# Moving VectorE's waits for transfers behind other work, and the scaling of the normed outputs to ScalarE, in a hybrid short-conv and gated DeltaNet layer

## The chip, the core and the metric

The kernel runs on one core of one Trainium2 chip. The metric is the device time of one execution in microseconds (us). A measurement of this kernel can tell differences of about 0.3% from no change.

## What is computed

One layer of a streaming encoder is applied to 4096 frames of a new stream and to 32 frames of a running stream. The reference, cut to what matters:

```python
h    = rmsnorm(x, ln_pre)                       # 4096 x 1024
proj = h @ w_in                                 # columns [B_a | C_a | X_a | Z_a | qkv | Z_g | a_dec | b_beta]
y_a  = b_a * causal_dwconv3(c_a * x_a) * silu(z_a)          # group A, 512 channels
q, k, v = split(silu(causal_dwconv4(qkv)))                  # group B, 4 heads x 128
q, k = l2norm(q), l2norm(k)
g    = -exp(a_log) * softplus(a_dec + dt_bias); beta = sigmoid(b_beta)
S_t  = exp(g_t) (I - beta_t k_t k_t^T) S_{t-1} + beta_t k_t v_t^T;   o_t = q_t^T S_t / sqrt(128)
y_g  = rmsnorm(o, gdn_norm_w) * silu(z_g)
y    = x + rmsnorm(concat(y_a, y_g) @ w_out, ln_post)
```

The outputs are both y, and the last inputs of the convolutions and the last state S of both streams.

## The kernel before, in words

The work has three stages. The first one (up to about 1400 us) goes over the stream in 16 blocks of 256 frames and makes group B. The second makes group A for eight pairs of blocks with a Winograd-like product of 2x2 blocks. The third multiplies by w_out and normalises. All matrix products use weights and activations split in two f16 parts, three products for one.

The first stage is written as a loop over groups, one block each. A group has eight steps (two pairs of k, q, v and z columns each, in the order k, k, q, q, v, v, z, z), and every step two slots, so a group has 16 slots. In a step TensorE makes two products of 24 matmuls (`proj`), ScalarE copies them out of PSUM (L430), ScalarE makes the first tap of the convolution (L434), VectorE the other three (L436, six instructions in a pair), and ScalarE the silu (L437). Other work of the block and of the block before it is put into numbered slots (`at_slot`, L858 on):

- `norm_qk`, `gram` and `subst` of the block at slots 7 to 12: the Gram products, their decayed copies M and at (L490, L491), a trip through DRAM (`lad`, `la`), the reciprocal of the diagonal on VectorE (L539 to L541), and a forward substitution of 31 steps on GpSimd (L546 to L551). Its result goes by 16 transfers (`Tc`, L560) into `merge`, at slots 26 to 31, that is in the next group.
- `gates` of the next block at slots 9, 10 and 13, and `decays` of the next block at the end of the group: a transfer of the cumulated gates to all partitions (`gB`, L397), one subtraction that waits for it (L398), eight instructions that make the exponents (L409), and their exponential on ScalarE (L404, L410).
- `xprep` of the next block at slot 2: norm, split and transposition of x (L271 to L299).
- `rec_a` and `rec_b` of the block before, slots 24 to 44: the recurrence over the state (L654, L674) and the output. `rec_b` adds the two halves of o (L687), squares it with an accumulated sum on ScalarE (L691), makes the norm's factor (L693, L694 on VectorE, a power on GpSimd at L137, called `rsqrt`, and the product with cc on VectorE at L696), scales o on VectorE (L697), transposes it on TensorE (`om`) and multiplies by the gate on VectorE (L703).
- `prep_a` at the fourth step: the weights of group A are made ready, a pair of columns in two halves. The first half (`scaled`) loads two tiles of w_in into `xtw` (L205), multiplies by ln_pre (L206, VectorE, waits for the transfer), takes absolute values on ScalarE (L208), adds them up (L213), sums over partitions on TensorE (`gL`), and scales by a power of two (L223 to L232). The second half (`out`, L749, L750) makes the sums and differences of the quarters on ScalarE and GpSimd.
- `prep_t` at the fourth step of groups 5, 6, 8, 9 and 11 to 14: sums of activations for the second stage, on GpSimd and ScalarE (L769 to L784).

Groups 1 to 13 call `prep_a` once, groups 4, 7 and 10 twice. First halves fall into groups 1, 3, 4, 6, 7, 9, 10 and 12, second halves into 2, 4, 5, 7, 8, 10, 11 and 13.

The order of the instructions on each engine is not the written one: a scheduler sorts them by dependence, by priority (`first` raises it) and by its own estimate of durations. `tc.issue_after(ins)` adds one more rule, that the instructions of the block that run on the engine of `ins` come behind it. Each engine then runs its list in order. All transfers are issued by SyncE. The transfers of `xtw` share five buffers (`xt`) with those of x.

Of the kernel before, what the change touches and what calls it, by code (L numbers as in the profile page):

```python
# [14 lines left out]
ALU = mybir.AluOpType  # L15
# [34 lines left out]
def hybrid_kernel(  # L50
# [139 lines left out]
    def scaled(cts, n=P, urow=None):  # L190


        ws = wa["w"] = []
        first = cts[0] >= 16
        nm = f"{cts[0]}"
        L = bank("r", [P, 2, P], f"L{nm}")[:, :len(cts), :n] if first else None
        sums = []
        e = te([P, 2, P], I32, "we", 1, nm)[:, :len(cts), :n]
        for i, ct in enumerate(cts):
            if 20 <= ct < 24:  # L200
                w = tl([P, D], F32, "v" if ct < 22 else "zg", 2, f"w{ct}")
            else:
                w = te([P, D], F32, "xt", NXT, f"w{ct}")
            w = w.rearrange("p (k c) -> p k c", k=KT)[:, :, :n]
            dma(w, w_in[:, ct * P:ct * P + n].rearrange("(k p) c -> p k c", p=P))  # L205
            (V if ct in VLN or not first else G).tensor_tensor(w, w, bc(lnp, 2, n), ALU.mult)  # L206
            ab = te([P, D], BF16, "jb", 1, f"w{ct}").rearrange("p (k c) -> p k c", k=KT)[:, :, :n]
            A.activation(ab, w, AF.Abs)  # L208
            kn = KT
            if not first:  # L210
                ab2 = e[:, i, 0:P // 2].bitcast(BF16)
                for kn, o in ((4, ab[:, 0:4]), (2, ab[:, 0:2]), (1, ab2.unsqueeze(1))):
                    V.tensor_tensor(o, ab[:, 0:kn], ab[:, kn:2 * kn], ALU.add)  # L213
                sums.append(ab2)
            for k in range(kn if first else 0):
                T.matmul(L[:, i], ones16, ab[:, k, :], start=k == 0, stop=k == kn - 1)
            ws.append(w)
        if not first:
            yield
            L = bank("g", [P, 2, P], f"L{nm}")  # L220
            for i in range(2):
                T.matmul(L[:, i], ones16, sums[i], start=True, stop=True)
        V.tensor_scalar(e.bitcast(F32), L, 2.0 ** -100, None, ALU.max)  # L223
        V.tensor_scalar(e, e, EXP_MASK, None, ALU.bitwise_and)
        if urow is not None:
            V.tensor_scalar(urow.bitcast(I32), e[:, 0], 1, float(-(WS + HS) * BIT), ALU.mult, ALU.add)
        else:
            u = te([1, 2, P], I32, "wu", 1, nm)
            V.tensor_scalar(u, e[0:1], 1, float(-(WS + HS) * BIT), ALU.mult, ALU.add)
        V.tensor_scalar(e, e, -1, float((254 + WS) * BIT), ALU.mult, ALU.add)  # L230
        for i, w in enumerate(ws):
            V.tensor_tensor(w, w, bc(e[:, i].bitcast(F32), 1, KT), ALU.mult)  # L232
        if not first:
            yield
        if urow is None:
            up = bank("o" if first else "g", [P, 2], f"u{nm}")
            for i in range(2):
                T.matmul(up[:, i:i + 1], u[:, i].bitcast(F32), one1, start=True, stop=True)
            V.tensor_copy(usc[:, cts[0]:cts[0] + 2], up)
# [181 lines left out]
    def qkv_pair(b, c0, dst):  # L421

        n = b["n"]
        pt = bank("pj", [P, 2, NB1], f"{b['id']}_c{c0}")
        proj(b, 16 + c0, pt[:, 0])
        yield
        proj(b, 17 + c0, pt[:, 1])
        u = te([P, 2, 3 + NB1], F32, "u", 2, f"{b['id']}_{c0}")
        V.tensor_copy(u[:, :, 0:3], b["hist"][:, c0:c0 + 2, :])
        A.activation(u[:, :, 3:3 + n], pt[:, :, :n], AF.Copy)  # L430
        V.tensor_copy(b["hist_new"][:, c0:c0 + 2, :], u[:, :, n:n + 3])
        for i in range(2):
            d = dst[:, i]
            A.activation(d, u[:, i, 0:n], AF.Copy, scale=cw[:, 0, c0 + i:c0 + i + 1])  # L434
            for j in range(1, 4):
                V.scalar_tensor_tensor(d, u[:, i, j:j + n], cw[:, j, c0 + i:c0 + i + 1], d, ALU.mult, ALU.add)  # L436
        queued("silu", lambda: A.activation(dst, dst, AF.Silu))  # L437

    def z_pair(b, c0):
# [81 lines left out]
    def subst(b):  # L521
# [14 lines left out]
            dma(la[32 * g:32 * g + nl], b["lad"].rearrange("c h q j i -> (c h q) j i"))  # L536

        rl = sc[:, 448:480]
        V.tensor_scalar(rl, la.rearrange("p a b -> p (a b)")[:, ::33], EPS, None, ALU.add)  # L539
        V.reciprocal(rl, rl)  # L540
        V.tensor_tensor(rl, rl, b["bl"], ALU.mult)  # L541
        G.memset(lt, 0.0)
# [135 lines left out]
    def rec_b(b, c):  # L678

        C = b["C"]  # L680
        nm = f"{b['id']}_{c}"
        sl = slice(c * C, (c + 1) * C)
        o, vn = b["rec"].pop(c)
        po = bank("m", [P, NH, P], f"o{nm}")[:C]
        for h in range(NH):
            T.matmul(po[:, h], b["at"][c][:, h, :C], vn[:, h], start=True, stop=True)
        V.tensor_tensor(o, o, po, ALU.add)  # L687
        so = tl([P, 2, NH], F32, "so", 2, nm)[:C]
        jk = b["at"][c]
        for h in range(NH):  # L690
            A.activation(jk[:, h], o[:, h], AF.Square, accum_out=so[:, 0, h:h + 1])  # L691
        f = so[:, 1]
        V.tensor_tensor(so[:, 0], so[:, 0], b["c2"][:, c], ALU.mult)  # L693
        V.tensor_scalar(so[:, 0], so[:, 0], EPS, None, ALU.add)  # L694
        rsqrt(so[:, 0], f)
        V.tensor_tensor(f, f, b["cc"][:, c], ALU.mult)  # L696
        V.tensor_tensor(o, o, bc(f, 2, P), ALU.mult)  # L697
        yield
        pm = bank("o", [P, NH, P], f"m{nm}")[:, :, :C]
        for h in range(NH):  # L700
            T.transpose(pm[:, h], o[:, h], ident[:C, :C])
        mg = b["zg"][:, :, sl]
        V.scalar_tensor_tensor(mg, pm, gwc, mg, ALU.mult, ALU.mult)  # L703
        if b["s"]:
            dma(mxd_s[:, NH:], mg)
        else:
            o0 = b["o"] + c * C
            dma(mxd[o0 // NB2][:, NH:, o0 % NB2:o0 % NB2 + C], mg)
# [157 lines left out]
    def run_slot(i):  # L866
        for fn in slots.pop(i, ()):
            fn()

    def first(fn, *a):  # L870

        with tc.high_priority(1500):
            fn(*a)
# [59 lines left out]
    for gi, grp in enumerate(groups):  # L933
# [5 lines left out]
        else:  # L939
# [19 lines left out]
            for si, (kind, c0) in enumerate(steps):  # L959
                ps = pair(b, kind, c0)  # L960
                next(ps)
                run_slot(s0 + 2 * si)
                ends(ps)
                run_slot(s0 + 2 * si + 1)
                if si == 3:
                    for _ in range((1 <= gi <= 13) + (gi in (4, 7, 10))):

                        p = prevs[-1]
                        with tc.issue_after(p["subst_end"]):
                            pa = prep_a()  # L970
                            if next(pa, 0) is None:
                                at_slot(s0 + 11, next, pa)
                                at_slot(s0 + 13, ends, pa)
                    if gi in (5, 6, 8, 9, 11, 12, 13, 14):
                        with tc.issue_after(prevs[-1]["subst_end"]):
                            prep_t((5, 6, 8, 9, 11, 12, 13, 14).index(gi))
        if gi + 1 < len(groups):
            decays(groups[gi + 1][0])
        for b in grp:
            if b["last"]:  # L980
                out_hist(b)
# [409 lines left out]
```

## Time and profile before

| | |
|---|---|
| median of 3 runs | 2385.7 us (2382.73 to 2390.21) |
| the profiled execution | 2385.77 us, of which the span of the trace is 2384.1 us |
| TensorE busy | 2141.4 us (90% of the span), 18626 matmuls |
| VectorE, ScalarE, GpSimd busy | 1564.8, 980.3 and 1333.7 us (66%, 41%, 56%) |
| mean granted clock of TensorE | 0.956 of full speed |
| chain of work that ended last | TensorE 15%, other engines 0% |

A matmul's end is modelled in this profile and matmuls overlap, so the busy time of TensorE says less than how many matmuls it starts in a microsecond. A wait is the idle time of an engine ahead of an instruction, put down to what came last.

### The profile page before, as it was taken

To read this page: it belongs to the slowest core of one execution; us is meant where nothing else is said; L and a number is where in the kernel's file an instruction comes from. 1 tells how busy PE (TensorE), PEld (TensorE's weight loads), DVE (VectorE), ACT (ScalarE), POOL (GpSimd) and SP (SyncE) were. 2 spreads that over 40 slices of the span, in tenths; PEclk is the share of its full clock that TensorE was granted. 3 is DMA by queue.
4 is the path that set the end of the run, shared out by engine and by line. 5 is a ranking of instruction groups with operands and counts; after the bars stand their busy time and mean duration, and the time that the engine had idled before them with its cause. 6 is when DMAs were issued, how large, how long until landed. Compare 5 with 4: busy or idle time off the path is not lost. (4 is left out here: it accounts for less than half of the span.)

```text
span 2384.1 us, 48173 instructions
## 1 busy us (share of the span) xinstructions
PE 2141.4 (90%) x18626; PEld 1713.9 (72%) x18626; DVE 1564.8 (66%) x3720; ACT 980.3 (41%) x2513; POOL 1333.7 (56%) x1750
## 2 busy tenths in 40 slices
PE   4676989799889988998899999899999999999998
PEld 3465878687778777877778889788888888444443
DVE  4786877677777786767766655656576656455661
ACT  4454655465556555655565411121221121333331
POOL 4435573656675767566776430674467431466763
PEclk9788999899899999999999999999999999999999
DMA  6344341433334243433342425212211122344441
GB/s 125 46 104 92 87 114 48 78 105 97 91 91 111 87 101 87 115 92 95 80 123 72 148 112 182 84 63 71 89 46 54 45 92 88 113 159 145 136 135 72
DMA packets 257198, 230.81 MB, mean 97 GB/s; under 512 B 111576, under 2 KB 196376, under 8 KB 256968
## 3 DMA queue, kind: packets, MB, share of 16 engines
q1 hardware_dynamic: 256968, 227.73, 33.9%
q8 instruction: 146, 2.39, 0.4%
q14 instruction: 84, 0.69, 0.1%
HBM read 133.09 MB, written 76.74 MB: 88 GB/s over the span
## 5 line engine op out<-in xcount | busy, mean ns | idle before, releaser
L74 PEld LDWEIGHTS <-w 128*128 128x128 f16 x6528 | 624.8, 101 | 117.7 <-POOL w L729 16.9
L74 PE MATMUL pj_c<-hhi,w 128*128 128x256 f16 x3072 | 559.6, 282 | 3.0 <-ACT u L430 3.0
L74 PE MATMUL pj_c<-hlo,w 128*128 128x256 f16 x1536 | 433.4, 282 | 0.0
L74 PEld LDWEIGHTS <-w_a 128*128 128x128 f16 x2880 | 269.5, 98 | 48.0 <-issue 16.0
L74 PEld LDWEIGHTS <-opm 128*128 128x128 f16 x1536 | 149.3, 98 | 176.2 <-issue 0.7
L551 POOL TENSOR_TENSOR lt<-lt 128x112 f32<-128x112 f32 (+29 forms) x496 | 235.4, 475 | 37.0
L436 DVE SCALAR_TENSOR_TENSOR qk<-u,cw,qk 128x256 f32<-128x256 f32 x384 | 238.5, 667 | 9.5 <-ACT qk L434 9.1
L550 POOL TENSOR_TENSOR lt<-la,lt 128x112 f32<-128x112 f32 (+29 forms) x496 | 211.6, 427 | 36.2
L74 PE MATMUL pja<-op,w_a 128*128 128x256 f16 x1536 | 190.0, 273 | 3.1 <-DVE w L1034 1.9
L74 PE MATMUL pj_z<-hhi,w 128*128 128x256 f16 x1024 | 187.9, 281 | 0.0
L74 PE MATMUL ga<-op,w_a 128*128 128x256 f16 x1152 | 147.7, 274 | 10.5 <-DVE w L1034 6.7
L74 PE MATMUL pj_z<-hlo,w 128*128 128x256 f16 x512 | 144.0, 281 | 0.0
L74 PE MATMUL pjo<-w_o,opm 128*128 128x512 f16 x528 | 118.5, 379 | 0.0
L137 POOL TENSOR_TENSOR oss<-oss,mhalf 128x2 f32<-128x2 f32 (+1 forms) x17 | 50.0, 2940 | 114.6 <-DVE oss L1280 114.6
L74 PE MATMUL ro<-w_o,opm 128*128 128x512 f16 x504 | 113.4, 379 | 0.0
L74 PE MATMUL go<-w_o,opm 128*128 128x512 f16 x504 | 113.1, 379 | 0.0
L546 POOL TENSOR_TENSOR la<-la,lt 128x1024 f32<-128x1024 f32 x16 | 38.0, 2374 | 126.9 <-DVE lt L541 103.6
L1034 DVE TENSOR_TENSOR w<-pja,w 128x256 f32<-128x256 f32 x152 | 61.7, 420 | 63.6 <-PE pja L74 61.5
L769 ACT ACTIVATE op<-tsc 128x512 f16<-128x512 f32 x48 | 30.2, 630 | 173.0 <-POOL tsc L775 100.0
L750 POOL TENSOR_TENSOR hl<-xtw,hl 128x512 f16<-128x512 f32 x56 | 66.7, 1208 | 61.9 <-ACT hl L749 61.9
L436 DVE SCALAR_TENSOR_TENSOR v<-u,cw,v 128x256 f32<-128x256 f32 x192 | 98.6, 549 | 3.0 <-ACT v L434 2.8
L437 ACT ACTIVATE qk<-qk 128x512 f32<-128x512 f32 x64 | 40.2, 633 | 142.8 <-DVE qk L436 142.8
(650 smaller groups left out, 4791.4 us busy)
## 6 DMA issues: line engine op xcount, KB each, us to landing
xt<-in_x_prompt_dram SPq DMA_DIRECT2D x32, 512.0 KB
mx<-mxd SPq DMA_DIRECT2D x16, 1024.0 KB
op<-hTd SPq DMA_DIRECT2D x30, 512.0 KB
xtw<-in_w_in_dram SPq DMA_DIRECT2D x28, 512.0 KB
wad<-hl SPq DMA_DIRECT2D x56, 256.0 KB
gB<-gd SPq DMA_DIRECT2D x16, 516.0 KB
hTd<-hhi SPq DMA_DIRECT2D x16, 512.0 KB
hTd<-hlo SPq DMA_DIRECT2D x16, 512.0 KB
```

The source lines that it names most:

```text
L74: return self.queue(nc.tensor.matmul(*a, **k))
L137: G.tensor_tensor(y, x, mhalf[:x.shape[0], :x.shape[-1]], ALU.pow)
L436: V.scalar_tensor_tensor(d, u[:, i, j:j + n], cw[:, j, c0 + i:c0 + i + 1], d, ALU.mult, ALU.add)
L437: queued("silu", lambda: A.activation(dst, dst, AF.Silu))
L546: E.tensor_tensor(la, la, bc(rl, 1, 32), ALU.mult)
L550: E.tensor_tensor(tm, bc(la[:, j, j + 1:32], 2, w), bc(lt[:, j, 0:w], 1, r), ALU.mult)
L551: last = E.tensor_tensor(lt[:, j + 1:32, 0:w], lt[:, j + 1:32, 0:w], tm, ALU.subtract)
L750: G.tensor_tensor(hl[:, 1], src, hl[:, 0], ALU.subtract)
L769: A.activation(d[i][0], t, AF.Copy)
L1034: V.tensor_tensor(dst, p, src, ALU.add)
```

## The change

Four things are changed. In `scaled`, both transfers are issued first, and for the weights of group A the generator then yields, so that the multiplication by ln_pre and the sums come in a later slot: 13 instead of the place in step four, behind the block's last Gram copy on VectorE (`behind`, `stage1_end`); the steps after them come at slots 17 and 19 (1 and 3 of the next group) instead of 11 and 13. In `subst` the first instruction that waits for `la` is put behind the last convolution of the pair before it (`conv_end`). `decays` of a block is called in the block's own group, after its first pair of k columns and behind that pair's last convolution on VectorE, instead of at the end of the group before. In `rec_b` the product with cc goes to GpSimd, and the scaling of o to ScalarE, as one instruction for each of the four heads.

```diff
@@ scaled
             dma(w, w_in[:, ct * P:ct * P + n].rearrange("(k p) c -> p k c", p=P))
+            ws.append(w)
+        if not first:
+            yield
+        for i, (ct, w) in enumerate(zip(cts, ws)):
+            ab = te([P, D], BF16, "jb", 1, f"w{ct}").rearrange("p (k c) -> p k c", k=KT)[:, :, :n]
             (V if ct in VLN or not first else G).tensor_tensor(w, w, bc(lnp, 2, n), ALU.mult)
-            ab = te([P, D], BF16, "jb", 1, f"w{ct}").rearrange("p (k c) -> p k c", k=KT)[:, :, :n]
             A.activation(ab, w, AF.Abs)
...
-            ws.append(w)
@@ qkv_pair
             for j in range(1, 4):
-                V.scalar_tensor_tensor(d, u[:, i, j:j + n], cw[:, j, c0 + i:c0 + i + 1], d, ALU.mult, ALU.add)
+                last = V.scalar_tensor_tensor(d, u[:, i, j:j + n], cw[:, j, c0 + i:c0 + i + 1], d,
+                                              ALU.mult, ALU.add)
+        b["conv_end"] = getattr(last, "ins", last)
@@ subst
-        V.tensor_scalar(rl, la.rearrange("p a b -> p (a b)")[:, ::33], EPS, None, ALU.add)
+        with tc.issue_after(b["conv_end"]):
+            V.tensor_scalar(rl, la.rearrange("p a b -> p (a b)")[:, ::33], EPS, None, ALU.add)
@@ rec_b
-        V.tensor_tensor(f, f, b["cc"][:, c], ALU.mult)
-        V.tensor_tensor(o, o, bc(f, 2, P), ALU.mult)
+        G.tensor_tensor(f, f, b["cc"][:, c], ALU.mult)
+        for h in range(NH):
+            A.activation(o[:, h], o[:, h], AF.Copy, scale=f[:, h:h + 1])
@@ the loop over groups
+    def behind(b, fn, *a):
+
+        with tc.issue_after(b["stage1_end"]):
+            fn(*a)
...
                 ends(ps)
+                if si == 0:
+                    with tc.issue_after(b["conv_end"]):
+                        decays(b)
...
                             if next(pa, 0) is None:
-                                at_slot(s0 + 11, next, pa)
-                                at_slot(s0 + 13, ends, pa)
+                                at_slot(s0 + 13, behind, b, next, pa)
+                                at_slot(s0 + 17, next, pa)
+                                at_slot(s0 + 19, ends, pa)
...
-        if gi + 1 < len(groups):
-            decays(groups[gi + 1][0])
```

The order that the scheduler makes of it, at three places. Lines of the changed kernel are a few numbers higher (L398 is L401, L409 is L412, L436 is L439, L697 is L704).

VectorE in group 9, in the second pair of k columns, before: the last number of a name tells tiles apart.

```order
L654 SCALAR_TENSOR_TENSOR R_1_10489<-rk_1_10719,sm_9192,R_1_10489 128x128 x4
L696 TENSOR_TENSOR so_0_10624<-so_0_10624,sm_9192 128x4
L697 TENSOR_TENSOR o_0_10067<-o_0_10067,so_0_10624 128x512
L206 TENSOR_TENSOR xtw_10864<-xtw_10864,lnp 128x1024
L431 COPY hist_10511<-u_6_10681 128x6
L436 SCALAR_TENSOR_TENSOR qk_10508<-u_6_10681,cw,qk_10508 128x256
L206 TENSOR_TENSOR xtw_10872<-xtw_10872,lnp 128x1024
L436 SCALAR_TENSOR_TENSOR qk_10508<-u_6_10681,cw,qk_10508 128x256 x2
L213 TENSOR_TENSOR jbw_10867<-jbw_10867 128x512
L703 SCALAR_TENSOR_TENSOR zg_8413<-om_0_10844,gwc,zg_8413 128x4x128
```

The same stretch now, from the first pair of k columns on:

```order
L660 SCALAR_TENSOR_TENSOR R_1_10534<-rk_1_10767,sm_9209,R_1_10534 128x128 x4
L293 SCALAR_TENSOR_TENSOR xth_0_10693<-xt_0_10685,xss_10684,xth_0_10693 128x1024
L293 SCALAR_TENSOR_TENSOR xth_128_10698<-xt_128_10688,xss_10684,xth_128_10698 128x1024
L434 COPY hist_10542<-u_4_10601 128x6
L439 SCALAR_TENSOR_TENSOR qk_10539<-u_4_10601,cw,qk_10539 128x256 x3
L710 SCALAR_TENSOR_TENSOR zg_8418<-om_0_10892,gwc,zg_8418 128x4x128
L439 SCALAR_TENSOR_TENSOR qk_10539<-u_4_10601,cw,qk_10539 128x256 x3
L401 TENSOR_TENSOR E_10445<-gB_10614 128x8
L432 COPY u_0_10810<-hist_9476 128x2x3
L412 SCALAR_TENSOR_TENSOR gB_10614<-gB_10614,E_10445,mneg 128x128
```

The two multiplications of `xtw` and the scaling of o are gone from here, the gate product of block 7 (zg) stands one pair of columns earlier, and the exponents of block 9 (gB) have come in behind the first pair's convolution; before, they stood ahead of it.

VectorE now, at the end of group 9, where the multiplications of `xtw` have gone:

```order
L495 TENSOR_TENSOR M_1_11293<-gq_1_11300,gB_10614 128x256
L496 TENSOR_TENSOR at_1_11294<-gq_1_11300,gB_10614 128x256
L211 TENSOR_TENSOR xtw_10912<-xtw_10912,lnp 128x1024
L211 TENSOR_TENSOR xtw_10914<-xtw_10914,lnp 128x1024
L439 SCALAR_TENSOR_TENSOR v_10540<-u_10_11204,cw,v_10540 128x256 x2
L519 TENSOR_TENSOR sm_11312<-beta_10425,r_11309 128x8
L522 TENSOR_SCALAR sm_11312<-r_11309 128x8
L217 TENSOR_TENSOR jbw_11485<-jbw_11485 128x512
L439 SCALAR_TENSOR_TENSOR v_10540<-u_10_11204,cw,v_10540 128x256 x2
```

They stand behind the block's last Gram copy and ahead of the last convolution of v; the instruction that waits for `la` follows nine rows later.

ScalarE now, at the start of group 9, with the new scaling of o (block 7, first half):

```order
L697 ACTIVATE at_0_9115,so_0_10669<-o_0_10112 128x128 x4
L292 ACTIVATE xth_0_10693<-xt_0_10685,xss_10684 128x1024
L292 ACTIVATE xth_128_10698<-xt_128_10688,xss_10684 128x1024
L666 ACTIVATE o_1_10781<-rq_1_10776,E_8310 128x128 x4
L704 ACTIVATE o_0_10112<-o_0_10112,so_0_10669 128x128 x4
L433 ACTIVATE u_4_10601<-pj_c_10545 128x2x256
L673 ACTIVATE vn_1_10853<-rv_1_10848 128x512
```

The scaling (L704) stands three entries behind the squares whose sum it needs, and ahead of the copy of the first pair of k columns out of PSUM (L433) and of vn, which the recurrence needs.

## Rows read from the trace of the kernel before

**Rows 1.** Busy time by stretch; the header names the columns (clock 1.00: full).

```profile
core 0: us, PE busy (x) PEld busy (x) DVE busy (x) ACT busy (x) POOL busy (x), PEclk, DMA share, GB/s
...
200.00:1294.00 1094.00, 965.70 (x9015) 828.97 (x9015) 785.75 (x2012) 609.26 (x1670) 692.26 (x1190) 0.94 0.36 92
```

**Rows 2.** The same for groups 2, 4, 5, 6, 10, 12, 13, 14.

```profile
268.14:336.65 68.51, 64.06 (x611) 54.62 (x609) 52.88 (x127) 39.10 (x112) 50.27 (x89) 0.95 0.30 92
...
414.63:503.93 89.30, 73.96 (x651) 62.39 (x650) 60.43 (x152) 44.28 (x121) 48.70 (x84) 0.87 0.39 90
503.93:582.88 78.95, 70.46 (x662) 60.14 (x660) 55.78 (x136) 43.55 (x123) 57.65 (x95) 0.96 0.34 95
582.88:663.31 80.43, 70.54 (x649) 60.64 (x648) 57.03 (x152) 43.49 (x119) 49.51 (x90) 0.92 0.39 96
...
902.76:983.87 81.11, 71.31 (x666) 62.12 (x664) 59.68 (x152) 46.01 (x124) 51.16 (x84) 0.94 0.40 99
...
1061.44:1140.79 79.35, 68.60 (x646) 59.01 (x644) 57.69 (x151) 42.62 (x119) 50.53 (x92) 0.96 0.38 97
1140.79:1219.62 78.83, 70.02 (x642) 59.17 (x640) 58.99 (x136) 42.76 (x119) 56.26 (x92) 0.94 0.32 92
1219.62:1294.01 74.39, 69.01 (x677) 59.91 (x675) 51.38 (x136) 43.97 (x127) 50.79 (x95) 1.00 0.33 79
sum 1025.87, PE 907.90 PEld 780.77 DVE 739.46 ACT 571.74 POOL 664.37; mean PE 69.84 PEld 60.06 DVE 56.88 ACT 43.98 POOL 51.11
```

**Rows 3.** The same view inside group 9.

```profile
839.00:859.00 20.00, 13.31 (x92) 10.70 (x91) 13.00 (x32) 7.88 (x20) 15.97 (x30) 0.83 0.61 155
859.00:902.76 43.76, 43.17 (x453) 37.22 (x452) 33.21 (x98) 27.17 (x85) 21.98 (x37) 1.00 0.26 74
```

**Rows 4.** Timeline, group 9: start, duration, operation, [idle before it, releaser].

```profile
846.89 1.24 DVE L206 TENSOR_TENSOR xtw<-xtw,lnp 128x1024 f32<-128x1024 f32 x1 [3.35 <-DMA xtw<-in_w_in_dram]
...
849.75 0.49 PE L74 MATMUL rS<-vn,kd 128*128 128x128 f32 x2 [3.21 <-ACT vn L667]
```

**Rows 5.** Waits of TensorE, 268 to 1294 us: total, times, longest.

```profile
PE gt L77 <- ACT qk L437: 29.5, 24, 3.8
PE om L77 <- DVE o L697: 25.3, 12, 7.0
...
PE m L74 <- DMA Tc<-la: 2.7, 4, 1.0
```

**Rows 6.** Waits of VectorE, 268 to 1294 us.

```profile
DVE xtw L206 <- DMA xtw<-in_w_in_dram: 47.9, 11, 10.0
DVE lt L539 <- DMA la<-lad: 41.7, 12, 5.7
DVE so L696 <- POOL so L137: 29.3, 17, 2.7
DVE E L398 <- DMA gB<-gd: 28.6, 13, 3.7
```

**Rows 7.** Waits, whole span, VectorE for the weights.

```profile
DVE xtw L206 <- DMA xtw<-in_w_in_dram: 59.5, 13, 10.0
```

**Rows 8.** Instructions by line and form, 268 to 1294 us: busy, mean ns, idle.

```profile
L409 DVE SCALAR_TENSOR_TENSOR gB<-gB,E,mneg 128x128 f32<-128x128 f32 x104 | 43.0, 482 | 0.4
...
L660 ACT ACTIVATE o<-rq,E 128x128 f32<-128x128 f32 x104 | 30.1, 381 | 1.5 <-PE rq L74 1.4
...
L697 DVE TENSOR_TENSOR o<-o,so 128x512 f32<-128x512 f32 x26 | 20.2, 777 | 0.3
...
L696 DVE TENSOR_TENSOR so<-so,sm 128x4 f32<-128x4 f32 x26 | 8.5, 328 | 29.3 <-POOL so L137 29.3
...
L551 POOL TENSOR_TENSOR lt<-lt 128x8 f32<-128x8 f32 x13 | 3.7, 285 | 1.0
```

**Rows 9.** Timeline of GpSimd: one step of the substitution in groups 9 and 10.

```profile
847.12 1.32 POOL L551 TENSOR_TENSOR lt<-lt 128x128 f32<-128x128 f32 x1
...
926.42 0.46 POOL L551 TENSOR_TENSOR lt<-lt 128x128 f32<-128x128 f32 x1
```

## The prediction

> **What bounds the kernel now.** I read the busy time by stretch first, then by group, then the waits of TensorE and VectorE, then the timeline of one group. The order of the program says where the change acts: the lists of all engines are the same up to about 200 us, and again behind the first stage, so only the 15 groups from 200 to about 1400 us can gain or lose. There TensorE starts 9015 matmuls in 1094 us at a granted clock of 0.94 [rows 1], 8.2 in a microsecond. How fast it goes when it is fed shows inside group 9: 453 matmuls in 43.76 us, 10.35 in a microsecond, at clock 1.00 [rows 3]. At that rate the 9015 would take 871 us, so some 220 us of the stretch are stalls and what the clock loses behind them. The end of the kernel is set by TensorE's queue, and TensorE waits in it for other engines.
>
> Where it loses them shows in the same rows: from 839 to 859 us it starts 92 matmuls in 20 us at clock 0.83 [rows 3]. At 10.35 these take 8.9 us, so 11.1 us of a group of 78.7 us go in one place. In this place VectorE sits 3.35 us ahead of the first multiplication of `xtw`, for the load of w_in, and TensorE 3.21 us for vn, which ScalarE makes behind the absolute value of that tile [rows 4]. Everything behind the wait in VectorE's list stands still with it: the convolution that the silu, and then the transposition gt, wait for (29.5 us of TensorE in 24 waits), and the scaling of o ahead of the transposition om (25.3 us in 12) [rows 5].
>
> **What the weight wait costs by group.** Groups differ in what `prep_a` and `prep_t` put into them [rows 2], which makes a comparison inside one trace. A first half beside `prep_t` (groups 6, 9, 12: 80.43 us the first, 79.35 the last, mean 79.5) against `prep_t` alone (group 14, 74.39): 5.1 us more. Both halves (4, 7, 10: 89.30 the first, 81.11 the last, mean 85.0) against a second half with `prep_t` (5, 8, 11, 13: 78.95 the first, 78.83 the last, mean 77.9): 7.1 us more. VectorE's waits for these loads are 47.9 us in seven groups [rows 6], 6.8 us a group, and 11.6 us more ahead of 268 us, in group 1 [rows 6, 7]. The rows also warn: groups without a first half still take 74 to 79 us, well above group 2's 68.51 us, so something else paces them.
>
> **The change, part by part.** *The weights.* The multiplications go from the middle of the convolutions to behind the last Gram copy. Both pairs of q columns and the first of v then lie between load and use, so the wait goes. In SyncE's list of group 9 the first of the two loads has come ahead of the transpositions of x; these are for the next group, and a load's delay of some microseconds hides in between. The work stays: two multiplications of 1.24 us [rows 4] now stand ahead of the instruction that waits for `la`. That one waits 41.7 us in 12 groups today [rows 6], 3.5 us each, which covers the 2.5 us; without this cover the substitution would start 2.5 us later in eight groups, 20 us at most. The sums and the scaling move on to the start of the next group, busy as long as before. What I credit is the difference by group: 5 us in groups 3, 6, 9 and 12, 7 us in 1, 4, 7 and 10: **48 us**. Ends: nothing, if what paces the other groups stands right behind; and 11.1 us in all eight, 89 us, if the whole hole of group 9 closes. I stay at the difference because the moved work and the other cause are in both sides of it.
>
> *decays and o.* VectorE loses four more things in the 13 groups from 268 us on: its wait for `gB`, 28.6 us (the transfer is issued at the same place of SyncE's list, behind `la` and the two small ones, and is used a pair of columns later); its wait for the power, 29.3 us [rows 6]; the product with cc, 8.5 us, and the scaling of o, 20.2 us [rows 8]. That is 86.6 us, 6.7 us a group. It counts only where VectorE is the last to come. VectorE is busy 739.46 of 1025.87 us [rows 2], so much of it would only make other idle time longer. I take a third, **29 us**: the waits for the power and the scaling of o lie on the way to om, the `gB` wait lies at the start of the group, where TensorE has two banks in hand. Ends: 0 and 86.6 us. The wait for `la` keeps its place in both lists, so that edit is worth nothing, and it hides behind the substitution's own start.
>
> *What is added.* ScalarE gets 26 times four instructions of the form of L660, 0.29 us apart (30.1 us for 104) [rows 8], 30 us in all. It is idle for 454 us of these groups [rows 2], and om needs only the first head to start, 0.29 us where the one instruction took 0.78 us: no cost, if the factor is there when ScalarE comes to it (second rival). GpSimd gets 26 small products; the trace has none of 128x4, the nearest are the last step of the substitution, 0.29 us [rows 8], and, as an upper end, a step that is held up, 1.32 us [rows 9]: 7.5 to 34 us. The former is nearer in size; they are put between steps of the substitution, and half of it counts, **4 us**.
>
> The exponents of `gB`, 104 instructions with 43.0 us [rows 8], now run later, beside the long steps of the substitution. That VectorE and GpSimd hold each other up shows in one step of it: 1.32 us in group 9, where the multiplication of `xtw` (846.89 to 848.13 us) runs beside it, 0.46 us in group 10, where none does [rows 4, 9]. The bounds for the move are 0 and the whole 43.0 us; I take a tenth, **4 us**, since these instructions already ran beside the first steps of the substitution and the `xtw` collisions, 0.9 us each, go away in exchange. The Trainium skill (SBUF — State Buffer, section "Who interferes with whom") speaks against me here: a VectorE instruction with both inputs in SBUF takes a read port that GpSimd also needs, and whoever comes first keeps it for the whole instruction. The step of 1.32 us agrees with it; by it the whole 43.0 us would count, and the sum would be that of the first rival.
>
> **The sum.** 48 + 29 - 4 - 4 = 69 us. The profiled execution took 2385.8 us, 0.1 us over the median of the runs shown, so the two need no correction: 2385.8 - 69 = **2317 us**, 2.9% faster.
>
> **The rivals.** *First: the substitution takes over.* GpSimd's forward substitution runs from the `la` wait until `merge`, and TensorE waits for its transfers `Tc` already now, though only 2.7 us in four groups [rows 5]: it is just in time. If TensorE comes to `merge` earlier and the exponents stretch the substitution by all of their 43.0 us, the gain is 48 + 29 - 4 - 43 = 30 us: 2356 us. For it: the small margin. Against it: the substitution itself gets rid of the `xtw` collisions and of the places where its power waited for a stalled VectorE.
>
> *Second, on the other side: ScalarE stands still for the factor.* Its list now has the scaling of o between the squares and the copy of the next columns out of PSUM. The power and the product are in GpSimd's list between steps of the substitution, and what VectorE waited for, 1.7 us a time (29.3 us in 17, the longest 2.7) [rows 6], ScalarE would wait for, plus one held-up step (1.32 us) and the product (0.29 us): 3.3 us at 26 places, 86 us, and with it vn, the copies and the silus of the convolution. Then 2385.8 - 69 + 86 = 2403 us. It decides from 69 / 26 = 2.7 us a place on. Against it: three entries stand between the squares and the scaling in the list of group 9, some work to fill the time, and ScalarE has the largest idle share.
>
> *Third: nothing comes of it.* The groups without first halves take 74 to 79 us although no load is waited for. If what paces them (the slow convolution of q beside GpSimd's `out` and `prep_t`) paces all, the waits taken away turn into waits for that, and the time stays at 2386 us, give or take 0.3%.
>
> **How the numbers follow.** Forecast 0.70, first rival 0.15, second 0.08, third 0.07. A difference of 0.3%, 7 us, is about what a measurement of this kernel can tell from none. Forecast and first rival are faster than that: 0.85; third the same: 0.07; second slower: 0.08. For the low end I take the weights at their upper end and half of VectorE's other relief: 89 + 43 - 8 = 124 us, 2262 us. The high end takes in the first rival with 12 us less from the weights: 2368 us. Outside lie the second and third rival and the tails.
>
> **What would show it.** If I am right, VectorE's waits for `xtw` and for the power are gone, TensorE's for om fall to a few microseconds, groups 6, 9 and 12 are as long as group 14 (73 to 75 us), and the clock from 200 to 1294 us rises above 0.94. Longer steps of the substitution and a larger wait for `Tc` mean the first rival; ScalarE idle ahead of L704 the second. I am wrong if the groups stay at 77 us or more on average, or if the time after 1400 us moves.

## The result, and the profile after

The changed kernel takes 2358.99 us (median of 4 runs, 2357.1 to 2364.23), the kernel before beside it 2387.95 us (median of 4, 2382.73 to 2390.49). The ratio is 0.9892, with a 95% interval of 0.9871 to 0.9913: faster by 1.1%. The profiled execution took 2357.1 us, its span is 2355.4 us. The forecast was 2317 us, so 26 us are saved (by the ratio) where 69 were expected.

| | before | after |
|---|---|---|
| TensorE, VectorE busy | 2141.4, 1564.8 us | 2135.7, 1539.2 us |
| ScalarE, GpSimd busy | 980.3, 1333.7 us | 1019.1, 1348.2 us |
| mean granted clock | 0.956 | 0.962 |

The first stage, by stretch; it answers to [rows 1]:

```profile
core 0: us, PE busy (x) PEld busy (x) DVE busy (x) ACT busy (x) POOL busy (x), PEclk, DMA share, GB/s
200.00:1294.00 1094.00, 980.59 (x9210) 846.25 (x9209) 775.10 (x1977) 653.79 (x1817) 727.43 (x1264) 0.95 0.37 94
```

In the same 1094 us TensorE starts 195 matmuls more, at a clock of 0.95 instead of 0.94. GpSimd is busy 35 us longer in them. Part of that is work that comes earlier now (over the whole execution it is 14.5 us more), and the only work that the change gives to GpSimd is the small product with cc.

The waits of VectorE and of TensorE, 268 to 1294 us (total, times, longest); they answer to [rows 5, 6]:

```profile
DVE hist L434 <- ACT u L433: 51.2, 32, 4.4
DVE qk L439 <- ACT qk L437: 36.6, 26, 5.3
...
DVE lt L545 <- DMA la<-lad: 21.8, 12, 4.9
```

```profile
PE om L77 <- ACT o L704: 35.4, 15, 6.9
PE gt L77 <- ACT qk L442: 19.7, 18, 3.4
...
PE m L74 <- DMA Tc<-la: 4.9, 5, 1.4
```

The three waits that the change aims at (for `xtw` 47.9 us, for the power 29.3, for gB 28.6) are gone from VectorE's list. In their place VectorE waits 88 us for copies and first taps that ScalarE makes. In the kernel before these two waits were 18 us:

```profile
DVE hist L431 <- ACT u L430: 14.3, 14, 2.3
...
DVE qk L436 <- ACT qk L434: 3.3, 6, 1.3
```

TensorE waits longer for om than before, 35.4 instead of 25.3 us, now for ScalarE's scaling.

By form, same stretch (busy, mean ns of one, idle before it):

```profile
L704 ACT ACTIVATE o<-o,so 128x128 f32<-128x128 f32 x108 | 34.5, 392 | 38.9 <-POOL so L702 38.9
...
L235 DVE TENSOR_TENSOR xtw<-xtw,we 128x1024 f32<-128x1024 f32 x16 | 20.6, 1327 | 0.1
...
L557 POOL TENSOR_TENSOR lt<-lt 128x152 f32<-128x152 f32 x14 | 13.7, 977 | 1.1
...
L702 POOL TENSOR_TENSOR so<-so,sm 128x4 f32<-128x4 f32 x27 | 10.6, 391 | 0.1
```

And from the kernel before:

```profile
L232 DVE TENSOR_TENSOR xtw<-xtw,we 128x1024 f32<-128x1024 f32 x14 | 16.5, 1210 | 0.0
...
L551 POOL TENSOR_TENSOR lt<-lt 128x152 f32<-128x152 f32 x13 | 7.3, 563 | 0.9
```

ScalarE stands still for 38.9 us ahead of its 27 scalings, because it waits for the factor. One instruction of the substitution, the subtraction of 128x152, takes 977 ns on average, where the same form took 563 ns before.

The length of the groups shows where time was won and lost. A group is measured here from the start of one substitution on GpSimd to the next, and the lengths are summed over groups of a kind:

| groups | before | after |
|---|---|---|
| 3, 6, 9, 12: first halves of `prep_a` alone | 325.5 us | 284.6 us |
| 4, 7, 10: both halves | 251.9 | 244.8 |
| 2, 5, 8, 11, 13: second halves alone | 373.8 | 402.6 |
| 14, 15 | 138.3 | 136.0 |

41 us are won in the groups that waited for the weights and have no late steps, and 29 us are lost in the groups that only hold the late steps. Group 8, one of those that lose, shows how. The rows give start, duration, operation and, in brackets, the idle time before it and the releaser. VectorE:

```profile
735.03 2.17 DVE L412 SCALAR_TENSOR_TENSOR gB<-gB,E,mneg 128x128 f32<-128x128 f32 x8
737.13 2.34 DVE L235 TENSOR_TENSOR xtw<-xtw,we 128x1024 f32<-128x1024 f32 x2
...
745.21 1.05 DVE L439 SCALAR_TENSOR_TENSOR qk<-u,cw,qk 128x256 f32<-128x256 f32 x2 [5.27 <-ACT qk L437]
```

GpSimd, ScalarE and TensorE in the same place:

```profile
735.16 4.68 POOL L557 TENSOR_TENSOR lt<-lt 128x152 f32<-128x152 f32 x1
...
741.38 1.01 POOL L137 TENSOR_TENSOR so<-so,mhalf 128x4 f32<-128x4 f32 x1
...
742.78 0.20 POOL L702 TENSOR_TENSOR so<-so,sm 128x4 f32<-128x4 f32 x1
```

```profile
743.01 1.28 ACT L704 ACTIVATE o<-o,so 128x128 f32<-128x128 f32 x4 [5.85 <-POOL so L702]
```

```profile
743.47 0.48 PE L77 MATMUL om<-ident,o 128*128 128x128 f32 x1 [6.95 <-ACT o L704]
```

A step of the substitution (here and below: one of its instructions) starts at 735.16 and ends only behind VectorE's ten instructions, 4.68 us later. The power and the product stand some steps behind it in GpSimd's list, so ScalarE comes to the scaling 5.85 us too early. ScalarE's first taps of the next columns stand behind the scaling in its list, so VectorE waits 5.27 us for them, and TensorE stands still 6.95 us ahead of om. The stretches around it, with the columns of the busy times above:

```profile
730.00:735.50 5.50, 5.47 (x50) 4.81 (x49) 5.50 (x18) 1.88 (x6) 4.95 (x8) 1.00 0.76 200
735.50:745.50 10.00, 3.05 (x20) 2.33 (x19) 4.73 (x12) 4.14 (x11) 9.37 (x13) 0.79 0.23 76
```

TensorE starts only 20 matmuls in these 10 us, and the granted clock goes from 1.00 to 0.79 with the hole. The first theory was the second rival of the prediction in a small form: moving the scaling of o to ScalarE makes ScalarE wait, and that eats the gain. Its rival was that the moved steps of the weights cost their time in the next group, whoever scales o.

### The profile page after: what moved, and what is told of

It reads as the page before. It is cut to its first block, busy times and chain, and to the rows that moved or that the text cites. A ratio compares the mean times of both kernels' runs of the same rounds, so it can differ in the third digit from the quotient of the medians.

```text
span 2355.4 us, 48294 instructions
## 1 busy us (share of the span) xinstructions
PE 2135.7 (91%) x18626; PEld 1710.4 (73%) x18626; DVE 1539.2 (65%) x3654; ACT 1019.1 (43%) x2646; POOL 1348.2 (57%) x1783
## 5 line engine op out<-in xcount | busy, mean ns | idle before, releaser
L74 PEld LDWEIGHTS <-w 128*128 128x128 f16 x6528 | 626.6, 101 | 115.7 <-POOL w L736 16.2
L74 PE MATMUL pj_c<-hhi,w 128*128 128x256 f16 x3072 | 572.1, 284 | 3.1 <-ACT u L433 3.1
L439 DVE SCALAR_TENSOR_TENSOR qk<-u,cw,qk 128x256 f32<-128x256 f32 x384 | 240.2, 676 | 42.7 <-ACT qk L437 42.7
L556 POOL TENSOR_TENSOR lt<-la,lt 128x112 f32<-128x112 f32 (+29 forms) x496 | 212.9, 429 | 35.4
L137 POOL TENSOR_TENSOR r<-ss,mhalf 128x16 f32<-128x16 f32 x16 | 47.1, 2946 | 122.5 <-DVE ss L514 77.9
L439 DVE SCALAR_TENSOR_TENSOR v<-u,cw,v 128x256 f32<-128x256 f32 x192 | 101.2, 558 | 3.4 <-ACT v L437 2.7
```

The costliest lines, as they stand in the source:

```text
L74: return self.queue(nc.tensor.matmul(*a, **k))
L137: G.tensor_tensor(y, x, mhalf[:x.shape[0], :x.shape[-1]], ALU.pow)
L439: last = V.scalar_tensor_tensor(d, u[:, i, j:j + n], cw[:, j, c0 + i:c0 + i + 1], d, ALU.mult, ALU.add)
L556: E.tensor_tensor(tm, bc(la[:, j, j + 1:32], 2, w), bc(lt[:, j, 0:w], 1, r), ALU.mult)
```

## The experiments

Savings below are worked out from the ratios: one per cent of the kernel before is 23.9 us. The intervals of the ratios are 0.002 to 0.003 to either side, or 4 to 7 us. Each series had its own runs of the kernel before beside it (medians 2384.6, 2386.0, 2387.3 and 2385.6 us).

**The parts alone.** The first run is the change with the two old lines in `rec_b`:

```diff
-        G.tensor_tensor(f, f, b["cc"][:, c], ALU.mult)
-        for h in range(NH):
-            A.activation(o[:, h], o[:, h], AF.Copy, scale=f[:, h:h + 1])
+        V.tensor_tensor(f, f, b["cc"][:, c], ALU.mult)
+        V.tensor_tensor(o, o, bc(f, 2, P), ALU.mult)
```

The other three are the kernel before with one of the parts alone: the edit of `rec_b`; the edits of `scaled` and of its slots 13, 17 and 19; the move of `decays`. The edit of `rl` (the instruction that waits for `la`) needed no run: without it the lists of all engines come out the same.

> The changed kernel with the scaling of o and its factor back on VectorE; the later weights and decays stay. Theory A (in the groups behind a first half, VectorE's gate exponents and weight scaling, back to back, hold up a step of GpSimd's substitution for some 4.7 us, the power comes late, and ScalarE stands still in front of the scaling of o): without ScalarE in the chain the stand-still costs VectorE alone, the second-half groups lose 3 to 5 us of their 82 to 86 us, the time is 2340 to 2352 us. Rival B (the weight steps that moved into the start of the next group cost their time there whoever scales o): second-half groups stay at 82 to 86 us, and the 28 us of VectorE work that come back make it 2360 to 2375 us. Rival C (the scaling on ScalarE is the part that brought the gain): 2375 us or more.

> The kernel before with only the scaling of o on ScalarE and its factor on GpSimd. Theory A: no late weight scaling and no gate exponents stand beside the power, so ScalarE waits little, some 1 us a place, and a few us are won: 2370 to 2386 us. Rival B says the same of this part. Rival C: 2360 us or less. If the scaling on ScalarE costs by itself in every group: 2395 us or more.

> The kernel before with only the weights of group A multiplied and scaled later. Theory A: the first-half groups win 7 to 15 us as in the changed kernel, and the weight scaling alone, without the gate exponents ahead of it and without ScalarE behind it, gives back 1 to 2 us a group: 2335 to 2350 us. Rival B: the second-half groups are 4 to 8 us longer all the same: 2358 to 2368 us. Rival C: 2375 us or more.

> The kernel before with only the gate exponents behind the first convolution of their own group. Theory A: VectorE no longer waits for the transfer (28.6 us), and the exponents meet the substitution; little moves: 2372 to 2390 us. If the exponents alone stretch the substitution by their whole 43 us: 2395 us or more. If the wait for the transfer lies on the path: 2360 us or less.

| | median | ratio, 95% interval | saved |
|---|---|---|---|
| e1, weights and decays | 2376.44 us | 0.9959 (0.9939 to 0.9978) | 10 us |
| e2, o alone | 2367.55 | 0.9918 (0.9891 to 0.9945) | 20 |
| e3, weights alone | 2379.79 | 0.9968 (0.9951 to 0.9985) | 8 |
| e4, decays alone | 2368.64 | 0.9933 (0.9913 to 0.9953) | 16 |

The first theory (A) falls: without the scaling on ScalarE the kernel is slower, not faster. The times of e1 and e3 lie where theory C, that the scaling on ScalarE brought the gain, put them, but e2 does not: o alone saves 20 us, less than C said. Theory B missed the times of e1 and e3, though the lengths of the groups are as it said: groups 5, 8, 11 and 13 take 82.0 to 85.1 us in e3, and 76.6 to 78.2 before. The part that disappoints is the weights, 8 us alone. With the weights alone the hole is there already, and VectorE is the one that waits for the power (waits, 268 to 1294 us; then the timeline of group 8):

```profile
DVE so L701 <- POOL so L137: 62.7, 17, 7.2
```

```profile
PE om L77 <- DVE o L702: 52.7, 16, 6.5
```

```profile
749.71 4.43 POOL L555 TENSOR_TENSOR lt<-la,lt 128x152 f32<-128x152 f32 x1
...
756.38 2.91 POOL L556 TENSOR_TENSOR lt<-lt 128x136 f32<-128x136 f32 x1
...
766.51 1.01 POOL L137 TENSOR_TENSOR so<-so,mhalf 128x4 f32<-128x4 f32 x1
```

```profile
751.49 2.34 DVE L235 TENSOR_TENSOR xtw<-xtw,we 128x1024 f32<-128x1024 f32 x2
...
767.55 0.25 DVE L701 TENSOR_TENSOR so<-so,sm 128x4 f32<-128x4 f32 x1 [7.17 <-POOL so L137]
```

The wait for the power has more than doubled, from 29.3 to 62.7 us, and the one for om too. The scaling of the weights (L235) again stands beside a step that is held up, 4.43 us. A second step is held up, for 2.91 us, beside the convolution (L439), so the weights are not the only work that does this. GpSimd's list is fixed, so all later steps, and the power between them, come late by as much: with half a microsecond for each of the two steps, they account for 6.4 of the 7.17 us that VectorE waits here.

**Taking the hold-up away.** Four variants of the whole change were run: without the weights part; with the late steps of the weights behind the substitution; with one operand of their scaling in PSUM; and with their steps at slots 13, 15 and 15. The edits of the second and the third follow; in the second, `behind` is given the name of the instruction to stand behind:

```diff
-                                at_slot(s0 + 17, next, pa)
-                                at_slot(s0 + 19, ends, pa)
+                                at_slot(s0 + 22, behind, b, next, pa, "subst_end")
+                                at_slot(s0 + 23, ends, pa)
```

```diff
-        V.tensor_scalar(e, e, -1, float((254 + WS) * BIT), ALU.mult, ALU.add)
+        es = e if first else L.bitcast(I32)
+        V.tensor_scalar(es, e, -1, float((254 + WS) * BIT), ALU.mult, ALU.add)
         for i, w in enumerate(ws):
-            V.tensor_tensor(w, w, bc(e[:, i].bitcast(F32), 1, KT), ALU.mult)
+            V.tensor_tensor(w, w, bc(es[:, i].bitcast(F32), 1, KT), ALU.mult)
```

> The whole change without the weights part: decays and o stay as changed, prep_a is as before. Theory T (the late steps of the weights, above all the scaling of xtw by VectorE beside the substitution, hold up GpSimd's steps and the power in their list, and so eat what their vanished wait gives): 2343 to 2354 us, faster than the whole change, and the steps of the substitution over 0.9 us fall from 62 us to about 50. Theory U (no harm in the late steps; the three parts only take the same idle time twice, so the whole change is as good as any two): 2356 to 2362. Theory V (the o part has cured what the late steps do, so the weights keep their gain of 5 to 8 us here): 2363 to 2370.

> The whole change with the sum over partitions and the scaling of the weights at slot 22, behind the end of the substitution on VectorE, instead of slots 17 and 19. T: no step of the substitution stands beside the scaling, the groups with only a second half of prep_a (2, 5, 8, 11, 13; 69.2 to 85.7 us with the whole change) come down by 3 to 6 us each, and the time is 2335 to 2350. U or V: the same work only stands elsewhere, 2354 to 2363; more than that if the second half of prep_a, which needs the scaled weights some slots later, now waits for them.

> The whole change, but the factor of the scaling of the weights is written to the PSUM bank of its sum, so that the two multiplications (L235) read one operand from SBUF and one from PSUM; their place in the list stays. T with the cause that both operands in SBUF keep GpSimd out: the steps of the substitution beside L235 last about as long as any other (before: 25.7 us over in 11 steps), 2340 to 2353. If it is only VectorE's time that counts, or if GpSimd is held all the same: 2354 to 2363.

> The whole change with the steps of the weights at slots 13, 15 and 15: the scaling stands behind the wait for la, at the start of the substitution, and so ahead of the first power and away from the exponents of gB (in the whole change they stand side by side). T: it still holds up the first steps of the substitution and the order of the power is no better, but the worst hold (4.7 us, exponents and scaling back to back) is split: 2345 to 2357. U: 2354 to 2363.

| | median | ratio, 95% interval | saved |
|---|---|---|---|
| e5, decays and o, no weights | 2369.71 us | 0.9932 (0.9909 to 0.9954) | 16 us |
| e6, scaling behind the substitution | 2335.84 | 0.9785 (0.976 to 0.9811) | 51 |
| e7, factor in PSUM | 2335.47 | 0.9784 (0.976 to 0.9809) | 52 |
| e8, scaling early | 2342.22 | 0.981 (0.9783 to 0.9837) | 45 |

Theory T, that the late steps hold up GpSimd and eat the gain, was wrong on the time of e5, which fell in the range of theory V: the weights part, harm and all, is still worth 10 us on top of the other two. On e6 to e8 it held in kind, and e7 and e8 came out faster than the ranges given for it. Two unlike edits, one that moves the late steps and one that changes only where an operand lies, give back the same 25 us. The step's form and ScalarE's wait, first with the scaling behind the substitution, and then TensorE's wait for om:

```profile
L704 ACT ACTIVATE o<-o,so 128x128 f32<-128x128 f32 x112 | 35.8, 396 | 16.2 <-POOL so L702 16.1
...
L557 POOL TENSOR_TENSOR lt<-lt 128x152 f32<-128x152 f32 x14 | 7.4, 525 | 1.0
```

```profile
PE om L77 <- ACT o L704: 22.8, 17, 3.5
```

Then with the factor in PSUM, by form, the wait for om, and VectorE and GpSimd in group 8:

```profile
L705 ACT ACTIVATE o<-o,so 128x128 f32<-128x128 f32 x112 | 35.7, 390 | 22.0 <-POOL so L703 22.0
...
L236 DVE TENSOR_TENSOR xtw<-xtw,gL 128x1024 f32<-128x1024 f32 x16 | 18.7, 1210 | 0.1
...
L558 POOL TENSOR_TENSOR lt<-lt 128x152 f32<-128x152 f32 x14 | 8.9, 637 | 1.1
```

```profile
PE om L77 <- ACT o L705: 16.7, 17, 2.5
```

```profile
726.04 2.35 DVE L236 TENSOR_TENSOR xtw<-xtw,gL 128x1024 f32<-128x1024 f32 x2
```

```profile
726.16 0.54 POOL L558 TENSOR_TENSOR lt<-lt 128x168 f32<-128x168 f32 x1
726.78 0.46 POOL L557 TENSOR_TENSOR lt<-la,lt 128x160 f32<-128x160 f32 x1
727.32 0.52 POOL L558 TENSOR_TENSOR lt<-lt 128x160 f32<-128x160 f32 x1
```

The same two multiplications take the same 2.35 us, and beside them GpSimd makes its steps in about half a microsecond each. In the whole change 11 steps over 0.9 us stand beside L235 and are 25.7 us longer together than 11 of 0.47 us (from the timelines of both engines, 262 to 1294 us). With the factor in PSUM there is none, with the scaling behind the substitution there are two, 1.5 us longer, and with the scaling early 16, 13.7 us longer: the hold-up is smaller, and so is the loss. Counted over all steps above 0.9 us, whatever stands beside them, the excess is 34.0 us before, 46.2 in the whole change, 23.1 in e6, 18.9 in e7 and 32.6 in e8. So what cost is not VectorE's time but GpSimd's. One caution: moving a step makes the scheduler move others too, in e7 as in the rest, so a single run of these could owe some microseconds to that.

**What the parts are worth when L235 holds nothing up.** Four more runs: the weights alone with the scaling behind the substitution ("clear"); the whole change with that cure (e6), once without the part in `rec_b` and once without the move of `decays`; and the whole change with both cures.

> The kernel before with the weights part alone, its sum over partitions and scaling at slot 22 behind the substitution. Theory A (the weight wait was worth about what the comparison of groups said, 34 to 48 us, and only the hold-up beside the substitution ate it): 2340 to 2354 us; the groups with a first half alone (3, 6, 9, 12) are 7 us or more shorter than before, those with a second half alone stay within 2 us. Theory B (the weights' gain needs the other two parts, since VectorE otherwise waits for the power or gB instead): 2362 to 2378, with VectorE's wait for the power above 29 us.

> The whole change with the late scaling (2335.8 us), and the scaling of o as before: product and scaling on VectorE. A (o and decays share one gain of some 16 us, as the run without the weights showed): 2336 to 2343. B: 2348 to 2360.

> The whole change with the late scaling, and decays at the end of the group as before. A: 2336 to 2343, and the exponents of gB no longer stand beside the long steps of the substitution. B: 2348 to 2360.

> The late scaling and the factor in PSUM together. If the hold beside the substitution was the whole harm, nothing is left to win by the second measure: 2330 to 2340. If the scaling behind the substitution still holds up GpSimd's halves of the weights (L755 and the like), up to 8 us better: 2326 to 2332.

| | median | ratio, 95% interval | saved |
|---|---|---|---|
| e9, weights clear, alone | 2364.8 us | 0.9909 (0.9888 to 0.993) | 22 us |
| e10, clear, without o | 2348.03 | 0.9847 (0.9821 to 0.9874) | 37 |
| e11, clear, without decays | 2351.33 | 0.9844 (0.9822 to 0.9866) | 37 |
| e12, clear, and factor in PSUM | 2333.68 | 0.9783 (0.9762 to 0.9803) | 52 |

Theory A falls and B holds for all three. In the clear, the weights alone give 22 us, decays or o another 15 each, and all of them 51. e12 is no faster than either cure alone, as it should be if there was one harm and each of them takes it away. The groups 2, 5, 8, 11 and 13 do not come back to their old length, though: they take 389.9 us in e6, and 373.8 before. With the weights alone VectorE waits for the power longer than before (29.3 us), though the steps beside L235 are held up by 1.5 us only. The other two parts take this wait away: it is 19.3 us with decays added (e10), and with o added (e11) VectorE has it no more:

```profile
DVE so L701 <- POOL so L137: 42.8, 21, 6.3
```

**Where the rest of the 48 us went.** The absolute values, sums and scaling of the weights of group A are left out, once in the kernel before and once in e9. The loads, the multiplication by ln_pre and the step that hands the factor on stay, with the factor set to 1; `return` leaves out what follows, the scaling with it:

```diff
-            A.activation(ab, w, AF.Abs)
             kn = KT
-            if not first:
+            if first:
+                A.activation(ab, w, AF.Abs)
+            if not first and False:
...
+            V.memset(u.bitcast(F32), 1.0)
...
+            return
```

> The kernel before, with the absolute values of the weights of group A, their sums and their scaling left out in all first halves (the factor is set to 1); the loads, VectorE's wait for them and the multiplication by ln_pre stay where they were. Theory W (the 5 to 7 us by which groups with a first half are longer are the wait and this work together; the change takes away the wait and moves the work): 2355 to 2372 us, and the groups 3, 6, 9 and 12 come down by 3 us or more. Theory X (they are the wait alone, the work hides): 2380 to 2390.

> The weights part alone with its late steps clear of the substitution (2364.8 us), and the same absolute values, sums and scaling left out. W: 2333 to 2350, that is wait and work together give the 48 us forecast for the wait, and the groups with a second half, which the moved work had made longer, are as before or shorter. X: 2358 to 2368.

e13 takes 2395.76 us, ratio 1.0039 (1.0017 to 1.0062): with less work it is 9 us slower than before. e14 takes 2353.1 us, ratio 0.9863 (0.9834 to 0.9892), 33 us saved. Theory W falls on the time of e13: leaving the work out of the kernel before saves nothing. Its sign for the groups came true all the same, since groups 3, 6, 9 and 12 come down from 325.5 to 309.8 us, but groups 4, 7 and 10 go up from 251.9 to 264.3 and groups 2, 5, 8, 11 and 13 from 373.8 to 382.7. What VectorE is spared it spends in longer waits for transfers, 54.0 us for `xtw` instead of 47.9 and 42.1 us for gB instead of 28.6:

```profile
DVE xtw L206 <- DMA xtw<-in_w_in_dram: 54.0, 9, 9.1
DVE E L404 <- DMA gB<-gd: 42.1, 13, 4.6
```

And the substitution is held up more than before, 47.6 us over in steps above 0.9 us (34.0 before), the increase being beside the multiplication by ln_pre and the convolution. So e13 is not only the kernel before with less work.

Behind the move the work does cost: e14, between the ranges of W and X, is 11 us faster than e9, and the groups 2, 5, 8, 11 and 13 together take 377.1 us in it, 409.7 in e9 and 373.8 before. What the wait alone is worth reads as 33 us, from the kernel before to e14, or as 42 us, from e13 to e14, neither of which has that work; the second contains what made e13 slow. How much of that is the order of its list stays open. Its clock in the first stage is the lowest of all:

```profile
200.00:1294.00 1094.00, 955.33 (x8851) 823.30 (x8849) 750.61 (x1911) 589.87 (x1644) 700.66 (x1187) 0.92 0.36 91
```

## Why the prediction was wrong, step by step

- **The bound.** Right. TensorE waits for other engines in the groups of the first stage, and the time from the last substitution to the end hardly moved (1028.8 us before, 1026.0 now).
- **The wait for the weights, 48 us.** Too large, but of the right order: 33 us where the work around it is left out, and 42 at most (e13, e14). Groups 6, 9 and 12 came to 72.9, 69.6 and 74.2 us, inside or under the 73 to 75 forecast for them; group 14 is at 71.1.
- **"The sums and the scaling move on to the start of the next group, busy as long as before."** This is the step that failed. It costed moved work at nothing, with no cover named. The reason given, that "the moved work and the other cause are in both sides" of the comparison by group, was false as well: groups with a first half were compared with groups without one, so the work of a first half stood on one side only. Before the change, leaving that work out saved nothing (e13, which also differs in other ways). Behind the change it costs 11 us even in the clear (e9 against e14), and about 25 us more beside the substitution (e6 and e7 against the changed kernel). With the weights moved alone, 8 us of the 48 are left (e3).
- **decays and o, 29 us.** Right in the clear: e9 to e6, 22 to 51 us, is 29. That the figure fits is partly luck: it was a third of what VectorE loses, and the reason given set little on the wait for gB, while decays and o turn out to be worth the same, 15 us each (e10, e11). Without the weights part they give 16 together, no more than either of them alone (e2 20, e4 16, e5 16).
- **The product on GpSimd, 4 us.** L702 is a small load by itself, 0.20 us in group 8 and 391 ns on average, 10.6 us in all, for which 7.5 to 34 us were forecast. What hurts more is its place, behind steps that are late. No run prices it alone.
- **The exponents beside the substitution, 4 us.** Nearly right by themselves: of the steps over 0.9 us in the changed kernel one, 1.4 us too long, stands mainly beside them. They make the hold longer where the scaling follows at once, as in group 8, where they fill about 2 of the 4.68 us, and that part is counted with L235. With the scaling out of the way two steps are held up mainly by them, 3.1 us, in e7 and none in e6. I weighed this collision for the exponents and not for the 16 long multiplications that the change moved to the same place; that `xtw` collides there too was in [rows 4, 9].
- **The sum.** 22 us (weights in the clear), plus 29 (decays and o), less 25 (hold-up) is 26, which is the measured saving. It is one chain of differences and has to close; what the runs add is the size of each link. The measured 2359 us lies inside the stated range, but at its slow end, which was set by the first rival, so the range says nothing for the mechanism of the forecast.
- **The first rival** (2356 us) came nearest in time, with half of its mechanism: the substitution is held up, but by the scaling more than by the exponents, and TensorE does not wait for `Tc` (4.9 us) but for om. The shared port was weighed against the change there. The Trainium skill (SBUF — State Buffer, section "Who interferes with whom") says that a VectorE instruction with at most one input in SBUF, and outside the two-port performance modes, does not contend with GpSimd. e7 agrees, with steps of 0.46 to 0.54 us beside 2.35 us of multiplications.
- **The second rival** was real but small: ScalarE stands still 38.9 us at 27 places, 1.4 us each, under the 2.7 us from which it would have decided. About half of it goes with the hold-up: it is 22.0 us with the factor in PSUM and 16.2 us with the scaling behind the substitution.
- **The signs named.** VectorE's waits for `xtw` and for the power vanished, and the clock rose to 0.95. But om's wait rose instead of falling, and groups 2 to 14 take 77.2 us on average (78.9 before), over the 77 us at which the text called itself wrong.

## What to carry to other kernels

Work that is moved has two prices, the one it had where it stood and the one it has where it goes; a stall that is about to be removed can have been the cover of the first. When work moves beside a serial chain on another engine, ask for each moved instruction, not only for the one you have in mind, whether the two engines share a resource, and what else stands in that chain's list behind the steps that are held up. A cure can be to move the work past the chain, or to keep the place and put one operand elsewhere: e6 and e7, at 2335.84 and 2335.47 us (ratios 0.9785 and 0.9784), beat both kernels.

## What the runs showed of the hardware

A GpSimd step that takes half a microsecond took 4.68 us beside ten VectorE instructions in a row with both inputs in SBUF, and 4.43 us beside a shorter run of seven: it ended only when the run had, not between two of its instructions. With one input in PSUM the same multiplications took as long (1210 ns against 1210 in the kernel before, 1327 in the changed one) and held up no step of the substitution. It is not always GpSimd that gives way. In e6, in group 8, the same eight exponents that took 2.17 us in the changed kernel take 3.65 us, and GpSimd's steps beside them take 0.43 to 0.52 us; VectorE, then GpSimd:

```profile
728.57 3.65 DVE L412 SCALAR_TENSOR_TENSOR gB<-gB,E,mneg 128x128 f32<-128x128 f32 x8
```

```profile
728.59 0.52 POOL L557 TENSOR_TENSOR lt<-lt 128x160 f32<-128x160 f32 x1
729.19 0.45 POOL L556 TENSOR_TENSOR lt<-la,lt 128x152 f32<-128x152 f32 x1
```

What decides which of the two gives way was not tested. And leaving work out made a kernel slower (e13): its traces show longer waits and hold-ups, and why its list came out that way is not known.
